# Pinning two weight-block sums behind the SwiGLU hand-over and moving the write-out of the residual stream

## The chip, the cores and the metric

The kernel runs on one core of a Trainium2 chip. The metric is device time in microseconds (us), the median over runs of the same program. One execution was also recorded by the hardware profiler; its own time is in the table below.

## The reference, cut to what matters

A trunk of two layers over 512 tokens of width 1024. Each layer is a half-step SwiGLU, a mixing block with three kinds of attention, and a second half-step SwiGLU. Every sub-layer sits between two RMS norms and adds to a residual stream `h`:

```python
def _swiglu(t, w_gate, w_up, w_down):
    return (jax.nn.silu(t @ w_gate) * (t @ w_up)) @ w_down
...
for l in range(DEPTH):                       # DEPTH = 2
    f = _swiglu(_rmsnorm(h, ffn1_pre_g[l]), ffn1_w_gate[l], ffn1_w_up[l], ffn1_w_down[l])
    h = h + 0.5 * _rmsnorm(f, ffn1_post_g[l])
    ...                                      # token mixing: h = h + _rmsnorm(merged @ w_out[l], mix_post_g[l])
    f = _swiglu(_rmsnorm(h, ffn2_pre_g[l]), ffn2_w_gate[l], ffn2_w_up[l], ffn2_w_down[l])
    h = h + 0.5 * _rmsnorm(f, ffn2_post_g[l])
```

The hidden width is 2816, 22 tiles of 128. Everything is float32.

## The kernel before, in words

**Products in three passes.** Each float32 operand is split into a high part (`wh`, `uh`: a cast on ACT, L180) and a low part (`wl`, `ul`: the rest, a subtraction on DVE, L181). A product is three matmul passes: high by high (L206), high by low (L207), low by high (L208). A weight block comes from DRAM into a `raw` tile by an SP DMA, then ACT makes its high part and DVE its low part. At most four high and four low weight tiles are live.

**A SwiGLU.** There are four, named a0, c0 (layer 0) and a1, c1 (layer 1). Each begins with the "first pair", hidden tiles 16 and 17, worked by `halved` in two halves over the tokens: the first half (tokens 0 to 255) starts as soon as token tiles 0 and 1 are normed and turned, the second (tokens 256 to 511) waits for tiles 2 and 3. Within a half, each weight is first used with the high part of the input (L639) and then with the low part (L636, L637). This second half is the hand-over.

After it the first 16 hidden tiles are worked as two chunks of seven block products each, for the gate (G), then the up weights (U). The seven products of a chunk use block-wise sums of inputs and of weights, in the order 0, 2, 1, 3, 4, 5, 6 (`ORDER`); each has two weight units (`k` = 0 and 2). A `BlockUnit` of product 2, 3, 5 or 6 needs a sum of two weight blocks first: one DVE `tensor_tensor` over 128x1024 (L316). For product 2 a second block is also fetched into a tile of the tag "o" that stays (`keep`; shown as `tga`, `tgc`, `tua`, ...).

The input side has sums too (`sums`, tiles `x..`, then `u` pairs), run on DVE beside the second half and the first four products.

**The chain to the second half.** For each token tile: residual add (L547), square sum on ACT, norm scale (L554), eight transposes on PE (L564), then the high part on ACT and the low part on DVE (L183, L184, tile `us_..`).

**Order.** The program is traced in the order the Python code runs, and a scheduler, which simulates the chip, then orders each engine's stream: an instruction goes when the simulation has its inputs ready, with the earlier traced one first among those that are ready. On the chip each engine then takes its stream in that order. `tc.keep_in_program_order(ins)` adds an edge that keeps `ins` behind the instruction traced last before it on the same engine. It adds no wait for a result.

At the start of the second half, `Q.load_ahead()` loads the next four units: the two of product 0 and the two of product 2 of chunk G 0. `Q.pinned` is true for that call, and `split` then pins the ACT cast and the DVE low part of each unit. The sum at L316 of product 2's units, traced just ahead of its cast, is not pinned.

**The tag "o" and the residual stream.** `h` lives in four of eight tiles of the tag "o". `leave()` writes the four tiles to DRAM (`park`, L650; not in a0, where `h` is still the input), and sets `RINGS["o"]` to 4, which lets `fetch_ahead` request weight blocks into the freed tiles. The write is read back at the SwiGLU's end.

The lines that the change touches lie in `BlockUnit.load` and in `halved`:

Of the kernel before, what the change touches and what calls it, by code (L numbers as in the profile page):

```python
# [13 lines left out]
ALU = mybir.AluOpType  # L14
# [8 lines left out]
def kernel(  # L23
# [38 lines left out]
    nc = tc.nc  # L62
# [47 lines left out]
    def pbank(tag, name):  # L110
        return ps.tile([P, S], F32, tag=tag, bufs=4, name=name)
# [121 lines left out]
    class Unit:  # L233
# [19 lines left out]
        def load(self):  # L253
            if self.h is not None:
                return
            self.fetch()
            self.split_from(self.raw[:])
            self.loaded()
# [16 lines left out]
    class BlockUnit(Unit):  # L275
# [31 lines left out]
        def load(self):  # L307
            if self.h is not None:
                return
            self.fetch()  # L310
            src = raw = self.raw[:]
            if self.n in (2, 3, 5, 6):
                t = self.keep.get(self.k0)
                src = raw if self.n == 5 else t
                a, b = (t, raw) if self.n in (2, 5) else (raw, t)
                nc.vector.tensor_tensor(src, a, b, ALU.subtract)  # L316
            self.split_from(src)
            self.loaded()

# [130 lines left out]
    Q = Queue()  # L450
# [138 lines left out]
    def ffn(l, src, wg, wu, wd, dst, name, spare, parked, plan, aside=None):  # L589
# [17 lines left out]
        def hidden(f, pg, pu):  # L607
            s = tmp(f"s{name}_{f}")
            nc.scalar.activation(s[:], pg[:], AF.Silu)
            if f < f0:  # L610
                nc.vector.tensor_tensor(hidden_rows(2 * f // FC)[:, f % (FC // 2)], pu[:], s[:], ALU.mult)
                return
            nc.vector.tensor_tensor(s[:], pu[:], s[:], ALU.mult)
            hid[f] = blk(tags[f - f0], f"hid{name}_{f}")
            split(hid[f][:, 0], hid[f][:, 1], s[:])
            if f == NF - 1:
                tc.keep_in_program_order(nc.scalar.preload_act_table_set("natural_log_exp_and_others"))

        def halved(f, ug, uu, half):
            if half == 0:  # L620
                st["p"] = [pbank("mm", f"p{x}{name}_{f + m}") for x in "gu" for m in range(2)]
            else:
                Q.hold, Q.pinned = False, True
                Q.load_ahead()
                Q.pinned = False
            c = HALVES[half]

            for uns, pts in ((ug, st["p"][:2]), (uu, st["p"][2:])):
                for low in (False, True):
                    for un in uns:  # L630
                        for k, (m, pt) in itertools.product(range(un.nk), enumerate(pts)):
                            kk, cols = un.k0 + k, slice(m * P, (m + 1) * P)
                            wh, wl = un.h[:, k, cols], un.l[:, k, cols]
                            ah, al = act(kk, c)
                            if low:
                                nc.tensor.matmul(pt[:, c], wh, al, start=False, stop=False, skip_group_check=True)  # L636
                                nc.tensor.matmul(pt[:, c], wl, ah, start=False, stop=kk == ND - 1, skip_group_check=True)  # L637
                            else:
                                nc.tensor.matmul(pt[:, c], wh, ah, start=kk == 0 and half == 0, stop=False, skip_group_check=True)  # L639
                            yield (1 + low) * S // 2 * PE_US  # L640
            if half == 1:
                for m in range(2):
                    hidden(f + m, st["p"][m], st["p"][2 + m])
                leave()

        def leave():

            if parked is not None:
                for t in range(NT):
                    nc.sync.dma_start(parked[t], hT[t][:])  # L650
            RINGS["o"] = 4
            Q.fetch_ahead()
# [206 lines left out]
        def first_pair():  # L859
            ug, uu = plain(f0)  # L860
            some = st["some"] = sums()
            marks["early"] = ug + uu
            for un, place in zip(ug + uu, ("tri", "tri", (spare, spare), (spare, spare))):
                un.tags = place
            Q.add(ug + uu, lambda: halved(f0, ug, uu, 0), src.ready((0, 1)))
            Q.add([], lambda: beside(halved(f0, ug, uu, 1), itertools.islice(some, 4), 12), src.ready(range(NT)))
            marks["first"] = len(Q.jobs)
# [751 lines left out]
```

## Time and profile before

| what | value |
|---|---|
| median of 3 runs | 2428.29 us (2422.43 to 2429.78) |
| profiled execution: its own time, its span | 2429.58 us, 2427.8 us |
| PE (matmul) busy | 2392.5 us, 99% |
| PE weight loads busy | 2134.2 us, 88% |
| DVE busy | 1870.4 us, 77% |
| ACT busy | 1365.0 us, 56% |
| DMA | 372.12 MB, mean 153 GB/s |

The span is the time from the first to the last instruction of the profiled execution. "Busy" is the time in which the engine has at least one instruction running. A row of the timeline is: start, duration, engine, line, operation, tile written <- tiles read, shapes, count, and in square brackets the engine's idle time before it with what ended it. SPq is the DMA queue of SyncE: there the duration is that of the issue, not of the transfer.

In the profiled execution the second halves of the four hand-overs start at about 27.4 us (a0), 884.2 us (c0), 1234.4 us (a1) and 2089.4 us (c1).

### The profile page before, as it was taken

How to read it: one execution, taken by the hardware profiler on the slowest of the kernel's cores; microseconds unless marked ns; L12 is line 12 of the kernel's file. 1: busy time of each engine (PE TensorE's matmuls, PEld its weight loads, DVE VectorE, ACT ScalarE, POOL GpSimd, SP SyncE). 2: the span in 40 equal slices, each digit the busy share in tenths (PEclk: the TensorE clock that was granted, in tenths of full speed). 3: DMA queues.
4: the chain of work that ended last, by engine and by line, in shares of the span. 5: the costliest groups of instructions: out<-in, count | busy, mean ns of one | idle time of the engine just before them, and what ended most of it. 6: DMA issues, size and time to landing. Idle time of an engine off the chain costs nothing.

```text
span 2427.8 us, 36744 instructions
## 1 busy us (share of the span) xinstructions
PE 2392.5 (99%) x14471; PEld 2134.2 (88%) x14471; DVE 1870.4 (77%) x2500; ACT 1365.0 (56%) x2201; POOL 70.9 (3%) x124
## 2 busy tenths in 40 slices
PE   9999999999999999999999999999999999999998
PEld 8998888888888889998899988888888888999886
DVE  8878876678776688788797788766778766887885
ACT  6555565567655555455554544655676655545544
POOL 0000000000110000000000000000001100000000
PEclk9999999999999999999999999999999999999999
DMA  6765454222223466655556655542232234576544
GB/s 235 225 195 186 157 192 138 77 72 70 79 70 113 153 203 196 213 175 177 193 187 215 198 184 173 185 118 70 71 87 75 65 129 150 190 230 196 177 158 151
DMA packets 249345, 372.12 MB, mean 153 GB/s; under 512 B 11450, under 2 KB 126162, under 8 KB 249172
## 3 DMA queue, kind: packets, MB, share of 16 engines
q1 hardware_dynamic: 249076, 369.74, 47.4%
q8 instruction: 114, 1.87, 0.3%
q14 instruction: 59, 0.48, 0.1%
q0 software_dynamic: 96, 0.03, 0.0%
HBM read 357.14 MB, written 12.58 MB: 152 GB/s over the span
## 4 chain that ended last, share of the span: by engine, by line
PE 78%; DVE 8%; DMA 7%; ACT 4%; issue 2%; SPq 0%; DVEq 0%; ACTq 0%
PE pg L206 3%; PE pg L207 3%; PE pg L208 3%; PE pdc L207 3%; PE pdc L206 2%; PE pdc L208 2%; PE pda L207 2%; PE pda L208 2%; PE pda L206 2%; PE pb L208 2%; PE pb L206 2%; PE pb L207 2%; DMA raw_da<-in_ffn_w_down_dram 1%; PE pwc0g L206 1%; PE pwc0g L207 1%
## 5 line engine op out<-in xcount | busy, mean ns | idle before, releaser
L206 PE MATMUL pg<-us_a,wh_wg 128*128 128x512 f32 x384 | 150.9, 393 | 0.0
L207 PE MATMUL pg<-us_a,wh_wg 128*128 128x512 f32 x384 | 150.0, 391 | 0.0
L208 PE MATMUL pg<-us_a,wl_wg 128*128 128x512 f32 x384 | 149.8, 390 | 0.0
L207 PE MATMUL pda<-wl_da,aha 128*128 128x512 f32 x224 | 87.5, 391 | 2.7 <-DVE wl_da L181 2.7
L207 PE MATMUL pdc<-wl_dc,ahc 128*128 128x512 f32 x224 | 87.6, 391 | 0.0
L208 PE MATMUL pdc<-wh_dc,alc 128*128 128x512 f32 x224 | 87.2, 389 | 0.0
L208 PE MATMUL pda<-wh_da,ala 128*128 128x512 f32 x224 | 87.2, 389 | 0.0
L206 PE MATMUL pda<-wh_da,aha 128*128 128x512 f32 x224 | 86.5, 389 | 0.0
L206 PE MATMUL pdc<-wh_dc,ahc 128*128 128x512 f32 x224 | 86.5, 389 | 0.0
L181 DVE TENSOR_TENSOR wl_dc<-raw_dc,wh_dc 128x1024 fp32r<-128x1024 f32 x50 | 61.1, 1222 | 32.2 <-ACT wh_dc L180 31.8
L208 PEld LDWEIGHTS pg<-us_a,wl_wg 128*128 128x128 f32 x384 | 72.4, 188 | 15.3
L206 PEld LDWEIGHTS pg<-us_a,wh_wg 128*128 128x128 f32 x384 | 72.4, 189 | 14.5
L207 PEld LDWEIGHTS pg<-us_a,wh_wg 128*128 128x128 f32 x384 | 72.4, 189 | 14.4
L180 ACT CAST wh_dc<-raw_dc 128x1024 fp32r<-128x1024 f32 x50 | 52.6, 1053 | 56.1 <-PE pdc L208 17.2
L184 DVE SCALAR_TENSOR_TENSOR wl_wg<-raw_wg,wh_wg 128x1024 fp32r<-128x1024 f32 x48 | 58.7, 1222 | 30.1 <-ACT wh_wg L183 29.8
L181 DVE TENSOR_TENSOR wl_da<-raw_da,wh_da 128x1024 fp32r<-128x1024 f32 x50 | 61.1, 1222 | 24.8 <-ACT wh_da L180 24.3
L180 ACT CAST wh_da<-raw_da 128x1024 fp32r<-128x1024 f32 x50 | 52.6, 1053 | 47.2 <-PE pda L208 19.7
L180 ACT CAST wh_uc<-raw_uc 128x1024 fp32r<-128x1024 f32 x44 | 46.2, 1049 | 50.7 <-PE pwc1u L207 10.7
L181 DVE TENSOR_TENSOR wl_uc<-raw_uc,wh_uc 128x1024 fp32r<-128x1024 f32 x44 | 53.7, 1221 | 24.7 <-ACT wh_uc L180 24.1
L180 ACT CAST wh_ua<-raw_ua 128x1024 fp32r<-128x1024 f32 x44 | 46.0, 1048 | 44.7 <-PE pwa1u L207 12.5
L181 DVE TENSOR_TENSOR wl_ua<-raw_ua,wh_ua 128x1024 fp32r<-128x1024 f32 x44 | 53.4, 1220 | 20.7 <-ACT wh_ua L180 19.9
L183 ACT ACTIVATE wh_wg<-raw_wg 128x1024 fp32r<-128x1024 f32 x48 | 51.0, 1062 | 28.2 <-PE pv L1043 16.2
(639 smaller groups left out, 8954.6 us busy)
## 6 DMA issues: line engine op xcount, KB each, us to landing
raw_da<-in_ffn_w_down_dram SPq DMA_DIRECT2D x74, 512.0 KB, 5.1
raw_dc<-in_ffn_w_down_dram SPq DMA_DIRECT2D x74, 512.0 KB, 4.8
raw_ga<-in_ffn_w_gate_dram SPq DMA_DIRECT2D x68, 512.0 KB, 4.6
raw_ua<-in_ffn_w_up_dram SPq DMA_DIRECT2D x68, 512.0 KB, 4.4
raw_gc<-in_ffn_w_gate_dram SPq DMA_DIRECT2D x68, 512.0 KB, 4.0
raw_uc<-in_ffn_w_up_dram SPq DMA_DIRECT2D x68, 512.0 KB, 4.3
raw_wg<-in_w_gate_dram SPq DMA_DIRECT2D x48, 512.0 KB, 3.6
raw_wo<-in_w_out_dram SPq DMA_DIRECT2D x24, 512.0 KB, 3.6
```

Source lines behind the costliest of these rows:

```text
L180: both = [nc.scalar.copy(h_ap, src)]
L181: make = lambda: nc.vector.tensor_tensor(l_ap, src, h_ap.bitcast(F32), ALU.subtract)
L183: both = [nc.scalar.activation(h_ap, src, AF.Copy, scale=scale)]
L184: make = lambda: nc.vector.scalar_tensor_tensor(l_ap, src, scale, h_ap.bitcast(F32), ALU.mult, ALU.subtract)
L206: nc.tensor.matmul(pt, lh, rh, start=start, stop=False, skip_group_check=free)
L207: nc.tensor.matmul(pt, lh, rl, start=False, stop=False, skip_group_check=free)
L208: nc.tensor.matmul(pt, ll, rh, start=False, stop=stop, skip_group_check=free)
```

## The change

Two edits. The sum of two weight blocks is pinned when `Q.pinned` is true, as the cast and the low part already are. And `leave()` is traced at the start of the second half, ahead of `Q.load_ahead()`, and no longer at its end.

```diff
@@ BlockUnit.load
                 a, b = (t, raw) if self.n in (2, 5) else (raw, t)
-                nc.vector.tensor_tensor(src, a, b, ALU.subtract)
+                ins = nc.vector.tensor_tensor(src, a, b, ALU.subtract)
+                if Q.pinned:
+                    tc.keep_in_program_order(ins)
             self.split_from(src)
@@ halved
             if half == 0:
                 st["p"] = [pbank("mm", f"p{x}{name}_{f + m}") for x in "gu" for m in range(2)]
             else:
+                leave()
                 Q.hold, Q.pinned = False, True
                 Q.load_ahead()
                 Q.pinned = False
@@ halved, at its end
             if half == 1:
                 for m in range(2):
                     hidden(f + m, st["p"][m], st["p"][2 + m])
-                leave()
```

## The prediction

> **What bounds the kernel now.** I read the page first, then the waits of PE, then the four hand-overs in the timeline, then windows over the stretch behind each.
>
> ```profile
> PE 2392.5 (99%) x14471; PEld 2134.2 (88%) x14471; DVE 1870.4 (77%) x2500; ACT 1365.0 (56%) x2201; POOL 70.9 (3%) x124
> ```
>
> PE sets the time: about 35 us of the span of 2427.8 are left in which it does nothing. A change that removes no matmul can win only what PE waits, and what a slow clock costs. At the hand-overs it waits here (PE, then DVE, in the timeline; c0, c1, a1):
>
> ```profile
> 889.06 0.38 PE L636 MATMUL pgc<-us_b,w_gc 128*128 128x256 f32 x1 [2.65 <-DVE us_b L184]
> 2093.19 0.39 PE L636 MATMUL pgc<-us_b,w_gc 128*128 128x256 f32 x1 [1.61 <-DVE us_b L184]
> 1228.81 0.41 PE L564 MATMUL utc<-ident,fc 128*128 128x128 f32 x2 [1.20 <-DVE nhc L470]
> ...
> 882.24 1.22 DVE L316 TENSOR_TENSOR tgc<-tgc,raw_gc 128x1024 f32<-128x1024 f32 x1
> 883.38 1.28 DVE L184 SCALAR_TENSOR_TENSOR us_b<-utb,us_b 128x512 fp32r<-128x512 f32 x2
> 887.17 1.23 DVE L316 TENSOR_TENSOR tgc<-tgc,raw_gc 128x1024 f32<-128x1024 f32 x1 [2.52 <-DMA tgc<-in_ffn_w_gate_dram]
> 888.32 1.28 DVE L184 SCALAR_TENSOR_TENSOR us_b<-utb,us_b 128x512 fp32r<-128x512 f32 x2
> ...
> 1226.24 1.23 DVE L316 TENSOR_TENSOR tga<-tga,raw_ga 128x1024 f32<-128x1024 f32 x1 [0.99 <-DMA raw_ga<-in_ffn_w_gate_dram]
> 1227.38 1.28 DVE L554 SCALAR_TENSOR_TENSOR fc<-hfc,nhc,gqc 128x1024 f32<-128x1024 f32 x1
> ```
>
> In c0 the second sum of the block weights (L316) stands in DVE's stream ahead of the low parts of token tile 3 (`us_b` at 888.32) and waits there 2.52 us for its own DMA. PE's low matmuls stand behind those low parts. In a1 the sum at 1226.24 stands ahead of tile 2's norm scale (L554), which PE's transposes need. So one cause shows three times: an early sum blocks a later, urgent instruction. a0 has the sum too, but no PE wait behind it (below).
>
> **The sums: what PE can gain.** With the pin the two sums come behind the low parts of product 0's units, which stand behind tile 3's low parts already, so none can stand ahead of `us_..`. Windows from the second half's first matmul to the start of its up weights (length first, granted clock third from the right; c0, c1, a1, then the slow part of c0):
>
> ```profile
> 884.20:894.50 10.30, 7.61 (x49) 7.41 (x50) 7.78 (x9) 5.69 (x7) 0.00 (x0) 0.83 0.75 226
> 2089.40:2097.30 7.90, 6.28 (x50) 6.08 (x51) 6.41 (x8) 5.71 (x7) 0.00 (x0) 1.00 0.71 224
> 1234.30:1240.20 5.90, 5.85 (x49) 5.85 (x49) 5.87 (x7) 5.59 (x7) 0.00 (x0) 1.00 0.41 127
> 889.00:894.40 5.40, 5.34 (x32) 5.35 (x33) 5.40 (x7) 1.76 (x2) 0.00 (x0) 0.68 0.80 232
> ```
>
> The same 48 matmuls take 5.9 us in a1, where nothing blocks `us_c`. So c0 can gain 10.3 - 5.9 = 4.4 us, c1 7.9 - 5.9 = 2.0; a1 gains its wait of 1.2; a0 nothing. That is a ceiling of 7.6 us. The 4.4 is more than the wait of 2.65: after it the clock was granted at 0.68 for 5.4 us, which costs 0.32 x 5.4 = 1.7 more. After the 1.61 of c1 it stayed at 1.00.
>
> [...]
>
> **The sums: what DVE gives back.** The sums are moved, not removed, and DVE behind the hand-over has no room. Windows from the end of tile 3's low parts to the low part of U 0's first weight unit (a0, c0, a1, c1; DVE busy is the fourth number):
>
> ```profile
> 28.95:76.01 47.06, 45.96 (x383) 45.76 (x383) 45.72 (x54) 34.10 (x42) 2.77 (x4) 1.00 0.65 212
> 889.60:934.88 45.28, 45.28 (x367) 45.28 (x366) 43.92 (x42) 24.05 (x29) 0.00 (x0) 0.96 0.61 200
> 1235.62:1281.02 45.40, 45.30 (x378) 45.09 (x376) 43.95 (x42) 27.36 (x34) 0.00 (x0) 1.00 0.45 143
> 2093.73:2138.55 44.82, 44.12 (x368) 43.91 (x366) 43.66 (x43) 24.94 (x30) 0.00 (x0) 1.00 0.62 204
> ```
>
> DVE idles 1.3, 1.4, 1.4 and 1.2 us in these 45 us. And PE meets DVE at their end:
>
> ```profile
> 931.39 2.35 DVE L316 TENSOR_TENSOR tuc<-tuc,raw_uc 128x1024 f32<-128x1024 f32 x2
> 933.66 1.22 DVE L181 TENSOR_TENSOR wl_uc<-raw_uc,wh_uc 128x1024 fp32r<-128x1024 f32 x1
> ...
> 935.04 0.28 PE L208 MATMUL pwc0u<-us_b,wl_uc 128*128 128x256 f32 x1
> ...
> PE pwa0u L206 <- ACT wh_ua L180: 1.1, 1, 1.1
> PE pwc1u L208 <- DVE wl_uc L181: 0.8, 1, 0.8
> PE pwa1u L208 <- DVE wl_ua L181: 0.2, 1, 0.2
> ```
>
> In c0 the low part ends at 934.88 and its matmul starts at 935.04; in a0, a1 and c1 PE already waits there. So up to this point the hand-over gains no more than DVE's stream moves forward. Two sums back to back take 933.66 - 931.39 = 2.3 us of that stream, which lay in its idle time before tile 3's low parts and now lie behind. How much earlier the low parts come is read against ACT, which makes their high parts (a1 is the free case; c0, c1, a1, a0):
>
> ```profile
> 883.59 1.08 ACT L183 ACTIVATE us_b<-utb 128x512 fp32r<-128x512 f32 x2 [2.05 <-PE utb L564]
> 2088.76 1.09 ACT L183 ACTIVATE us_b<-utb 128x512 fp32r<-128x512 f32 x2 [2.07 <-PE utb L564]
> 2092.45 1.28 DVE L184 SCALAR_TENSOR_TENSOR us_b<-utb,us_b 128x512 fp32r<-128x512 f32 x2
> 1233.70 1.08 ACT L183 ACTIVATE us_c<-utc 128x512 fp32r<-128x512 f32 x2 [3.14 <-PE utc L564]
> 1234.33 1.29 DVE L184 SCALAR_TENSOR_TENSOR us_c<-utc,us_c 128x512 fp32r<-128x512 f32 x2 [2.57 <-ACT us_c L183]
> 26.71 1.09 ACT L183 ACTIVATE us_x<-utx 128x512 fp32r<-128x512 f32 x2 [4.83 <-PE utx L564]
> 27.67 1.28 DVE L184 SCALAR_TENSOR_TENSOR us_x<-utx,us_x 128x512 fp32r<-128x512 f32 x2
> ```
>
> Free, DVE follows ACT by 1234.33 - 1233.70 = 0.63. So c0's low parts can start at 884.22 and not 888.32 (4.1 earlier), c1's at 2089.39 and not 2092.45 (3.1), a0's 0.3 earlier; a1's move with PE by 1.2. Less 2.3 each: c0 +1.8, c1 +0.8, a1 -1.1, a0 -2.0, together -0.5 us: a small loss. Against it, a stream that PE waits for closes idle time: at most all of the 1.3 + 1.4 + 1.4 + 1.2 = 5.3 us, which gives a gain of 4.8. I take half, since part of that idle time hangs on PE, which comes earlier, and part on DMAs, which don't: c0 +2.5, c1 +1.4, a1 -0.4, a0 -1.3, a gain of 2.2 us. Each is below its ceiling from PE.
>
> **What waits behind the pinned sums.** ACT's cast of product 2's units and DVE's low parts of them; then, as far as the simulation lets nothing pass, the input sums. The one round trip the trace shows is this:
>
> ```profile
> 888.43 1.05 ACT L180 CAST wh_gc<-tgc 128x1024 fp32r<-128x1024 f32 x1 [0.94 <-DVE tgc L316]
> ```
>
> From the sum's end at 888.40 to the cast's end at 889.48 are 1.1 us, twice per hand-over, since the second sum is pinned behind the first unit's low part. I count it at nothing: the input sums over `us_b` are ready then and are not pinned, so the scheduler can fill in. Without that cover it is the second rival.
>
> **The residual stream.** `leave()` issues four writes on SP in c0, a1 and c1 (none in a0), and its `fetch_ahead` the block fetches on the same queue; nothing of it is on POOL, ACT or DVE.
>
> ```profile
> 878.84 0.34 SPq L650 DMA_DIRECT2D park<-hm  x1
> 883.20 0.37 SPq L294 DMA_DIRECT2D tgc<-in_ffn_w_gate_dram  x1
> 883.68 0.41 SPq L294 DMA_DIRECT2D raw_gc<-in_ffn_w_gate_dram  x1
> ...
> 903.24 1.06 ACT L180 CAST wh_gc<-raw_gc 128x1024 fp32r<-128x1024 f32 x1 [1.63 <-PE pwc0g L207]
> ```
>
> The last write goes out at 878.84, 5.4 us ahead of the second half at 884.2, though it is traced behind it: it only waits for the residual add. Its landing frees the tile for the `keep` block at 883.20. Tracing it earlier changes none of these waits, and the fetches behind it are the same in the same order. Product 1's first block, fetched at 883.68 into a tile that the first sum frees, will be fetched some 5 us later, when that sum now ends; its cast at 903.24 waits for PE, not for the fetch. So I count nothing, between a gain and a loss of 4 x 0.34 = 1.4 us of SP issue time per hand-over, were the order on SP to turn.
>
> **Rivals.** First, the full gain: the scheduler, with the sums out of the way, orders DVE so that the low parts PE meets come ahead of sums needed later. The row at 931.39 speaks for it: two sums for U's product 2 stand ahead of the low part that PE needs at once. Against it: the same order came out in c0 and c1. Gain 7.6 us, 2420.7.
>
> Second, slower: the pinned chain sum, cast, low part, sum, cast, low part runs with nothing between, and DVE idles 2 x 1.1 = 2.2 us in each hand-over. Then c0 is -0.4, c1 -1.4, a1 -3.3, a0 -4.2, together 9.3 us lost, or 6.6 with the half of the idle time closed: 2434.9 to 2437.6. It decides where the input sums are already done or not ready when the first sum ends; nearest to it is a0, whose constants and input sums run first.
>
> Third, the pin moves nothing in the real stream, or as much is lost as won: 2428.3.
>
> **How the numbers follow.** The profiled execution took 2429.58 us, 1.8 more than its span and 1.3 more than the median of 2428.29. The span should become 2427.8 - 2.2 = 2425.6, and the median of runs 2426.1; the forecast's own range is 2423.5 to 2428.8. A measurement of this kernel tells about 0.3% (7.3 us) from no change: faster means below 2421.0, slower above 2435.6.
>
> Chances: the forecast 0.43 (0.04 of it faster, 0.39 within), the full gain 0.30 (0.20 faster, 0.10 within, since 2420.7 lies on the edge and the scheduler may shift other streams a little), the alternating chain 0.22 (0.16 slower, 0.06 within), nothing 0.05 (0.01 faster, 0.02 within, 0.02 slower). That is 0.25, 0.57 and 0.18. The range goes from 2418 (the full gain, and 2.7 below it for the scatter of runs, which spans 7 us) to 2437.
>
> **What would show it.** Right: L316 on `tgc<-tgc` behind the `us_..` low parts at all four hand-overs; no PE wait on `us_b L184`; clock 1.00 there in c0; second halves of 5.9 us; and a PE wait on U 0's `wl_u..`/`wh_u..` that grows in each SwiGLU, most in a0. The first rival: that wait gone or unchanged, and DVE's `tu.` sums behind `wl_u.`. The second: DVE idle 1 us before `wl_g.<-tg.` with ACT `wh_g.` as releaser, twice per hand-over. Wrong: PE waits of a new kind, on DMA blocks of product 1 or 3, or a different order on SP between `park` and the fetches.

## The result, and the profile after

The changed kernel takes 2415.1 us (median of 8 runs, 2410.15 to 2418.79) against 2425.98 us of the kernel before (median of 8, 2422.43 to 2429.78): 10.9 us less, ratio 0.9957, 95% interval 0.9945 to 0.9968. The prediction was 2426.1 in a range from 2418 to 2437, so the gain is five times the forecast's 2.2 us. The interval, 7.8 to 13.3 us, lies just above the 7.6 us that the prediction called a ceiling.

The profiled execution after took 2410.15 us, 4.95 below its own median, while that of before lay 3.6 above its median. So 8.5 of the 19.4 us between the two spans are the scatter of executions. The two traces can't simply be subtracted; what follows is read hand-over by hand-over. Page of the changed kernel, span, busy time and chain:

```profile
span 2408.4 us, 36758 instructions
...
PE 2385.7 (99%) x14471; PEld 2130.9 (88%) x14471; DVE 1871.3 (78%) x2500; ACT 1365.9 (57%) x2201; POOL 70.9 (3%) x124
...
PE 87%; DVE 6%; DMA 3%; ACT 2%; issue 1%; SPq 0%; DVEq 0%; ACTq 0%
```

PE is idle for 2408.4 - 2385.7 = 22.7 us, where it was 35.3. The waits of PE (in all, times, longest):

```profile
PE pts L1082 <- ACT ts L1111: 5.0, 2, 2.6
PE utc L566 <- DVE fc L556: 2.6, 1, 2.6
PE pda L207 <- DVE wl_da L181: 2.0, 3, 0.9
PE warm L1483 <- DVE warm L1575: 1.2, 1, 1.2
```

The waits for `us_b L184` are gone, and so are those for `wl_u..` and `wh_u..` at U 0. Windows over the second half of c0, c1, a1 and a0, from its first matmul to the first of its up weights:

```profile
877.14:882.99 5.85, 5.85 (x49) 5.85 (x50) 5.85 (x7) 3.64 (x5) 0.00 (x0) 1.00 0.49 131
2074.70:2080.55 5.85, 5.85 (x48) 5.85 (x49) 5.85 (x7) 3.64 (x5) 0.00 (x0) 1.00 0.37 112
1221.42:1227.27 5.85, 5.85 (x48) 5.85 (x49) 5.85 (x7) 3.64 (x5) 0.00 (x0) 1.00 0.22 59
26.48:32.27 5.79, 5.79 (x50) 5.79 (x49) 5.53 (x13) 2.26 (x3) 1.16 (x1) 1.00 0.82 307
```

All four take the 5.8 to 5.9 us of an undisturbed one, at a granted clock of 1.00. DVE in c0, from tile 3's low parts on:

```profile
877.12 1.29 DVE L184 SCALAR_TENSOR_TENSOR us_b<-utb,us_b 128x512 fp32r<-128x512 f32 x2 [0.89 <-ACT us_b L183]
878.32 1.22 DVE L688 TENSOR_TENSOR x10c<-us_b 128x1024 f32<-128x1024 f32 x1
879.46 2.36 DVE L181 TENSOR_TENSOR wl_gc<-raw_gc,wh_gc 128x1024 fp32r<-128x1024 f32 x2
881.73 1.22 DVE L316 TENSOR_TENSOR tgc<-tgc,raw_gc 128x1024 f32<-128x1024 f32 x1
882.86 1.22 DVE L688 TENSOR_TENSOR x11c<-us_b 128x1024 f32<-128x1024 f32 x1
...
886.27 1.22 DVE L181 TENSOR_TENSOR wl_gc<-tgc,wh_gc 128x1024 fp32r<-128x1024 f32 x1
887.40 1.22 DVE L316 TENSOR_TENSOR tgc<-tgc,raw_gc 128x1024 f32<-128x1024 f32 x1
```

The low parts start 0.63 us after ACT's high parts (which start at 876.49), as in the free case of before, the two sums stand behind product 0's low parts, and other ready work fills the time of the cast between a sum and its low part: input sums (L688) behind the first, a low part of the input side and a product of the first pair behind the second, with no idle time shown. Now the stretch from the end of tile 3's low parts to U 0's first low part (a0, c0, a1, c1):

```profile
27.69:72.47 44.78, 44.78 (x375) 44.78 (x374) 44.52 (x52) 29.03 (x37) 2.76 (x4) 1.00 0.58 187
878.41:923.24 44.83, 44.83 (x376) 44.83 (x375) 44.66 (x43) 27.18 (x33) 0.00 (x0) 1.00 0.64 208
1222.69:1267.52 44.83, 44.83 (x376) 44.83 (x375) 44.66 (x44) 27.19 (x33) 0.00 (x0) 1.00 0.48 151
2075.97:2120.81 44.84, 44.84 (x376) 44.84 (x375) 44.67 (x44) 27.19 (x33) 0.00 (x0) 1.00 0.61 199
```

PE is busy for all of it, so it is PE's own work that sets these 44.8 us. DVE idles 0.2 to 0.3 us (44.83 - 44.66 in c0) instead of 1.2 to 1.4. At its end DVE reads:

```profile
920.88 1.22 DVE L316 TENSOR_TENSOR tuc<-tuc,raw_uc 128x1024 f32<-128x1024 f32 x1
922.02 1.22 DVE L181 TENSOR_TENSOR wl_uc<-raw_uc,wh_uc 128x1024 fp32r<-128x1024 f32 x1
...
924.51 1.23 DVE L181 TENSOR_TENSOR wl_uc<-raw_uc,wh_uc 128x1024 fp32r<-128x1024 f32 x1
925.65 1.22 DVE L316 TENSOR_TENSOR tuc<-tuc,raw_uc 128x1024 f32<-128x1024 f32 x1
```

Before, both sums of the up side's product 2 stood ahead of the low part that PE meets. Now one stands ahead and one behind, in a1 and c1 too; in a0 both are behind.

Setting the start of each matmul after against the same one before gives the gain by hand-over: a0 1.4 us, c0 4.4, a1 1.7, c1 2.8, in all 10.3, which is the 10.9 us of the medians within their scatter. a0 is counted from 26 us on. The changed trace is 0.45 us ahead by 14.6 us already, but the first instruction with another place in the order comes only at 23 us, so that is scatter; the expectations below, with 1.9 us for a0 and 10.4 in all, count it in. Of the remaining 9 us between the two traces, the largest pieces (at 117, 229, 383 and 396 us, together 5.2) lie in places whose instruction order did not change.

### The profile page after: what moved, and what is told of

Read it like the earlier page. It is cut to its first block, busy times and chain, and to the rows that moved or that the text cites. A ratio compares the mean times of both kernels' runs of the same rounds, so it can differ in the third digit from the quotient of the medians.

```text
span 2408.4 us, 36758 instructions
## 1 busy us (share of the span) xinstructions
PE 2385.7 (99%) x14471; PEld 2130.9 (88%) x14471; DVE 1871.3 (78%) x2500; ACT 1365.9 (57%) x2201; POOL 70.9 (3%) x124
## 4 chain that ended last, share of the span: by engine, by line
PE 87%; DVE 6%; DMA 3%; ACT 2%; issue 1%; SPq 0%; DVEq 0%; ACTq 0%
PE pg L206 3%; PE pg L207 3%; PE pg L208 3%; PE pdc L207 3%; PE pdc L208 3%; PE pdc L206 3%; PE pda L207 2%; PE pda L208 2%; PE pda L206 2%; PE pb L208 2%; PE pb L206 2%; PE pb L207 2%; PE pwo L207 1%; PE pwo L206 1%; PE pwo L208 1%; DMA raw_da<-in_ffn_w_down_dram 1%
## 5 line engine op out<-in xcount | busy, mean ns | idle before, releaser
L184 DVE SCALAR_TENSOR_TENSOR wl_wg<-raw_wg,wh_wg 128x1024 fp32r<-128x1024 f32 x48 | 58.7, 1222 | 30.2 <-ACT wh_wg L183 29.9
L180 ACT CAST wh_da<-raw_da 128x1024 fp32r<-128x1024 f32 x50 | 52.7, 1053 | 46.2 <-PE pda L208 19.4
```

Of the source, the lines that this page charges most:

```text
L180: both = [nc.scalar.copy(h_ap, src)]
L184: make = lambda: nc.vector.scalar_tensor_tensor(l_ap, src, scale, h_ap.bitcast(F32), ALU.mult, ALU.subtract)
```

## The experiments

Each ratio is to the kernel before on the same chip, with its 95% interval.

**Which of the two edits.** First the sums pinned, `leave()` left where it was:

```diff
-                nc.vector.tensor_tensor(src, a, b, ALU.subtract)
+                ins = nc.vector.tensor_tensor(src, a, b, ALU.subtract)
+                if Q.pinned:
+                    tc.keep_in_program_order(ins)
```

> The sums kept in program order, the residual write left where it was. Theory A (the pinned sums carry the whole gain, 1.9 us at a0, 4.2 at c0, 1.5 at a1 and 2.8 at c1, 10.4 in all): the ratio to the kernel before is 0.9957 (0.9945 to 0.997), and TensorE waits for no us_ tile at any hand-over. Theory B (the earlier residual write carries part of it, by freeing the queue or the tiles ahead of the second half): at least 3 us of the 10.9 are missing, 0.997 or more.

Measured: 0.9959 (0.9946 to 0.9971). The order on PE, DVE, ACT and POOL is that of the full change; on SP one block fetch and one write of the residual are exchanged at c0, a1 and c1. The four stretches are 44.8 us again, and no wait for tile 3's low parts of `us_` is left. Theory A holds. The other edit alone:

```diff
             else:
+                leave()
                 Q.hold, Q.pinned = False, True
...
-                leave()
```

> The residual write ahead of the second half, the sums left free. Theory A: 1.000 (0.999 to 1.001), with the waits of 2.65 us at c0 and 1.61 us at c1 for us_b still there. Theory B: 0.9988 or less, that is 3 us or more gained without the pin.

Measured: 1.0003 (0.9994 to 1.0012), nothing gained. The free sum blocks in c0 once more, only a place earlier: DVE holds it for its DMA ahead of the norm scale, so the wait is PE's for `fb` this time, and the expected 2.65 us for `us_b` shows as 1.95 here. In c1 the expected 1.61 us shows as 0.54 for `fb` and 0.62 for `us_b`, and the wait for `wl_uc` at U 0 rises from 0.76 to 1.68 us. DVE, then PE, in c0:

```profile
880.57 1.23 DVE L316 TENSOR_TENSOR tgc<-tgc,raw_gc 128x1024 f32<-128x1024 f32 x1 [1.51 <-DMA raw_gc<-in_ffn_w_gate_dram]
...
883.34 1.06 PE L564 MATMUL utb<-ident,fb 128*128 128x128 f32 x8 [1.95 <-DVE fb L554]
```

**One hand-over alone.** The kernel before with the pin in a0 only:

```diff
+                if Q.pinned and self.name.startswith('ga0'):
+                    tc.keep_in_program_order(ins)
```

> The kernel before with the pin at a0's hand-over alone. Theory A: 1.9 us gained, ratio 0.9992 (0.9987 to 0.9997), with the activation-table loads at 67 to 79 us of the kernel before gone from that place. Rival (what a0 showed was scatter between executions): 1.0000 (0.9997 to 1.0003) and the waits near 19, 26 and 75 us still there.

Measured: 0.9990 (0.9981 to 0.9998), that is 2.4 us. The interval is too wide to tell 1.4 us from 4, but it excludes that nothing was gained, and the prediction had a0 losing 1.3. The trace, set against that of before from 26 us to U 0, gives 1.4 us again. The kernel before has six loads of an activation table on ACT between 67 and 80 us, three of them ahead of U 0's first cast. Here the first load of that stretch comes at 79.6 us, behind U 0, and the wait of 1.10 us for `wh_ua` is gone. Is that the loads, or DVE? The next kernel moves the loads and leaves the sums at the hand-over where they were:

```diff
-            nc.scalar.activation(ss[:, 1:2], ss[:, 0:1], AF.Ln)
+            tc.keep_in_program_order(nc.scalar.activation(ss[:, 1:2], ss[:, 0:1], AF.Ln))
```

> The kernel before with the Ln activations of mem_norm kept in program order, which takes ScalarE's table loads out of the stretch from 60 to 80 us and leaves the sums as they were. Theory A2 (1.24 us of a0's gain came from these loads having moved, not from the sums themselves): the wait of 1.10 us of TensorE for wh_ua at unit 0 of a0 is gone, while the waits near 19 and 26 us, 0.5 us each, stay. Rival (the sums at the hand-over decide it through VectorE): the wait of about 1.1 us at unit 0 stays.

Measured, in a single run: 2428.07 us, and the wait for `wh_ua` is gone; U 0 starts at 73.62 instead of 74.79, 1.2 us earlier. So of a0's gain some 1.2 us can be had without the pin, with the loads of 1.28 us each gone from there. Three of them stood in ACT's stream ahead of the cast that U 0 needed, and the pin moved them as a by-product of the new order. The loads were not the only thing that moved, though: in this kernel too the second sum of the up side stands behind U 0's low part (73.33 against 72.20 us), and its DVE does not wait for the block of that sum. What the loads are worth alone is not shown.

**How much room DVE has.** The changed kernel with each pinned sum followed by one more operation that leaves it as it is:

```diff
                 if Q.pinned:
                     tc.keep_in_program_order(ins)
+                    tc.keep_in_program_order(nc.vector.tensor_tensor(src, src, src, ALU.max))
```

> The changed kernel with one more VectorE operation of 128x1024 (a maximum of the sum with itself, which changes nothing, about 1.2 us) behind each pinned sum: two at each hand-over, eight in all. Theory C (VectorE's backlog up to unit 0 has no slack left, so that what the sums push back is paid again at unit 0): 2.3 us come back at each of the four, 9 us in all, and the ratio is 0.9995 (0.9985 to 1.0005), with a wait of about 2 us at unit 0's first low part. Theory D (the scheduler closes the backlog: other work that is not due is put behind unit 0's low part, as it did with the second sum): the stretch from the end of the us_ low parts to unit 0 stays within 0.5 us of 44.8 us at all four, and the ratio is 0.9957 to 0.997.

Measured: 1.0005 (0.9996 to 1.0014). All of the gain is lost, as theory C has it, but not where it said. The stretches of a0, c0, a1 and c1, and the rows on PE and DVE in c0:

```profile
27.29:75.49 48.20, 45.47 (x377) 45.06 (x376) 47.94 (x54) 28.99 (x37) 2.76 (x4) 1.00 0.58 187
886.69:933.46 46.77, 45.15 (x377) 44.95 (x375) 46.77 (x45) 26.73 (x33) 0.00 (x0) 1.00 0.63 204
1235.85:1282.62 46.77, 45.15 (x376) 44.95 (x375) 46.77 (x46) 26.74 (x33) 0.00 (x0) 1.00 0.48 148
2092.39:2139.16 46.77, 45.16 (x377) 44.96 (x376) 46.77 (x46) 26.73 (x33) 0.00 (x0) 1.00 0.60 196
...
920.81 1.22 DVE L181 TENSOR_TENSOR ulc<-x11c,uhc 128x1024 fp32r<-128x1024 f32 x1
922.08 0.38 PE L207 MATMUL pwc0g<-ulc,wh_gc 128*128 128x256 f32 x1 [1.62 <-DVE ulc L181]
...
118.46 0.39 PE L208 MATMUL pwa0g<-us_x,wl_ga 128*128 128x256 f32 x1 [2.25 <-DVE wl_ga L181]
1323.96 0.38 PE L208 MATMUL pwa1g<-us_c,wl_ga 128*128 128x256 f32 x1 [0.62 <-DVE wl_ga L181]
2180.48 0.38 PE L208 MATMUL pwc1g<-us_b,wl_gc 128*128 128x256 f32 x1 [0.60 <-DVE wl_gc L181]
```

DVE has no idle time left in c0, a1 and c1, and of 2.3 us more they lose 46.77 - 44.9 = 1.9 in this stretch, at an input of the gate side's products, not at U 0. a0 loses 3.4. PE also waits at the next block of weights (the last three rows; in c0 0.41). Only in a0 is that more than scatter: kernels without the extra work have waits of 0 to 0.7 us there in c0, a1 and c1 as well. Half of the extra work, behind the second sum only:

```diff
+                    if self.k0 == 2:
+                        tc.keep_in_program_order(nc.vector.tensor_tensor(src, src, src, ALU.max))
```

> The changed kernel with one more VectorE operation of about 1.2 us at each hand-over, behind the second pinned sum only. With two of them, 2.3 us of work lengthened the stretch from the us_ low parts to unit 0 by 1.9 us at c0, a1 and c1, and TensorE waited for ulc or ula, not for unit 0. Theory I (VectorE had 0.4 us left ahead of that input in the changed kernel): 1.15 - 0.4 = 0.75 us comes back at each hand-over, the stretch is about 45.65 us instead of 44.9, with a wait of 0.5 to 0.8 us for ulc; about 3 us in all, ratio 0.9969 (0.9957 to 0.998). Rival (the scheduler's other order with two operations made the wait, and the room is larger): 44.9 us at all four and 0.9957.

Measured: 0.9975 (0.9965 to 0.9984), nearly the predicted ratio, and again not in the predicted places:

```profile
28.52:77.92 49.40, 46.91 (x377) 46.50 (x375) 47.34 (x53) 28.72 (x37) 2.76 (x4) 0.97 0.57 181
889.50:934.40 44.90, 44.90 (x377) 44.90 (x376) 44.76 (x43) 26.98 (x33) 0.00 (x0) 1.00 0.62 201
1234.98:1279.88 44.90, 44.90 (x377) 44.90 (x376) 44.76 (x43) 26.96 (x33) 0.00 (x0) 1.00 0.47 144
2088.65:2133.55 44.90, 44.90 (x377) 44.90 (x375) 44.77 (x43) 26.96 (x33) 0.00 (x0) 1.00 0.60 193
```

c0, a1 and c1 take 1.15 us more without any loss, with other work again put behind the low part: theory I falls there, and its rival holds. Only a0 loses. Of its 49.40 us 1.7 are a slow clock that followed its waits in this execution (3.4 us at 0.50, hence the mean of 0.97), which leaves a loss of 2.9 us, about as much as with twice the work (48.20, a loss of 3.4). So the cost of pushed-back work is no fixed amount. In three of four places 1.15 us cost nothing and 2.3 us nearly all of it; in a0 1.15 us cost more than itself, and why a0 has no room was not followed.

Then the U sums of product 2 pinned as well, on top of the sums done twice:

```diff
-                if Q.pinned:
+                if Q.pinned or self.name[0] == 'u' and self.n == 2:
                     tc.keep_in_program_order(ins)
```

> The kernel with the sums done twice, and the sums of the up side's product 2 kept in program order as well, which puts unit 0's two low parts ahead of one more of them. Theory H (what VectorE can put behind unit 0's low part decides how much of a hand-over's pushed-back work is paid): 1.1 us less is paid at each of the four unit 0s than with the sums done twice alone, the stretch from the us_ low parts to unit 0 falls from 46.8 to about 45.6 us, and the ratio is 0.9986 (0.9975 to 0.9998). Rival (unit 0 is bound by ScalarE's casts or by the landing of the up weights): the stretch stays at 46.8 us and the ratio at 1.0005.

Measured: 0.9986 (0.9977 to 0.9996), the expected ratio, but not by the expected way. A window of c0, then a row of a0:

```profile
884.93:931.71 46.78, 45.16 (x377) 44.96 (x375) 46.16 (x44) 26.75 (x33) 0.00 (x0) 1.00 0.63 204
...
118.03 0.38 PE L208 MATMUL pwa0g<-us_x,wl_ga 128*128 128x256 f32 x1 [1.25 <-DVE wl_ga L181]
```

The stretch to U 0 is as long as without this pin, so theory H falls: U 0's low part was not what PE waited for. Between the two traces the wait at the next block is shorter: 2.25 us became 1.25 in a0, 0.60 became 0.19 in c1, those of c0 and a1 (0.41 and 0.62) are gone, and a0's drop of the clock (0.50 from 120.6 to 123.8 us with the sums done twice, below) did not come: here it stays at 1.00 from 112 to 132 us. That adds up to 4 of the 4.6 us between the two ratios, but it is one execution against one, and waits of 0 to 0.7 us come and go there between executions of one order. What brought the ratio back is not settled.

**The clock.** The changed kernel with 4, 5 and 6 more operations ahead of tile 3's low parts in c0, a1 and c1 (in the edit `b0`, `c0` and `b1`, the chains that lead to them), to lengthen PE's wait:

```diff
+                if hf == 0 and t == NT - 1:
+                    for _ in range({'b0': 4, 'c0': 5, 'b1': 6}.get(self.name, 0)):
+                        tc.keep_in_program_order(nc.vector.tensor_tensor(self.fs[t][:], self.fs[t][:], self.fs[t][:], ALU.max))
```

> The changed kernel with four (c0), five (a1) and six (c1) more VectorE operations of about 1.2 us, which change nothing, ahead of tile 3's low parts. TensorE should wait about 2.5, 3.6 and 4.8 us for us_ at the three hand-overs. Theory E (the length of the idle decides on the granted clock, and the bound lies between the 2.56 us that a1 waited at 1.00 and the 2.65 us that c0 of the kernel before waited before 0.68): the second halves of a1 and c1 run at 0.6 to 0.7 for some 5 us and take 7.2 us or more instead of 5.9, c0's stays at 1.00. [...]

Measured, in a single run: 2441.28 us. The waits came out 3.82, 5.08 and 6.34 us, longer than planned, and all three were followed by a clock of 0.50 (c0, the time after it, a1, c1):

```profile
885.10:891.80 6.70, 5.73 (x25) 5.36 (x26) 4.77 (x6) 3.76 (x4) 0.00 (x0) 0.50 0.09 9
891.90:895.20 3.30, 3.30 (x30) 3.30 (x30) 2.87 (x3) 1.14 (x2) 0.00 (x0) 1.00 0.96 342
1240.00:1246.80 6.80, 5.07 (x22) 4.70 (x23) 4.87 (x5) 3.76 (x4) 0.00 (x0) 0.50 0.00 0
2100.20:2110.40 10.20, 6.26 (x28) 5.89 (x29) 8.20 (x8) 3.76 (x4) 0.00 (x0) 0.50 0.09 15
```

The slow stretches last 6.8, 6.8 and 10.2 us. They begin 3.4 us after the wait of c0 began (881.57), 4.0 after that of a1 and 3.1 after that of c1. Theory E's bound between 2.56 and 2.65 us does not exist: other runs have a clock of 0.50 behind a wait of 1.71 us and of 1.00 behind one of 2.84 (last section).

**The wait that is left at a1.** The changed kernel with a1's first up units in another ring of tiles:

```diff
+            if name == 'a1':
+                for un in uu:
+                    un.place = 'v'
```

> The changed kernel with a1's up units of the first pair fetched into another ring of tiles. Theory G (the wait of 2.6 us that is left ahead of a1's transpositions comes from VectorE standing at wl_ua, whose weights land late because their tile comes free late): that wait falls under 0.7 us and the ratio to the kernel before is 0.995 (0.9937 to 0.9962). Rival (the norm's own chain is as long): the wait stays above 2 us, 0.9957.

Measured: 0.9937 (0.9925 to 0.9949), with this wait left:

```profile
1210.09 1.09 PE L566 MATMUL utc<-ident,fc 128*128 128x128 f32 x8 [1.05 <-DVE fc L556]
```

2.6 us became 1.05: less than theory G wanted, more than its rival allows. The next two kernels ran side by side, the change unaltered, and the ring with the U sums pinned:

> The changed kernel unaltered, beside the next one on the same chip: 0.9957 (0.9945 to 0.9968). It is there to tell whether the variant with another ring for a1's up units (0.9937) is faster than the change itself: then this one stays 2 us or more above it; if the two were the same, this one comes out at 0.9937 to 0.995 as well.

> The changed kernel with a1's up units of the first pair in the other ring and the sums of the up side's product 2 in program order as well. If the ring takes the wait of 2.6 us ahead of a1 to about 1.1 us and the pin brings nothing where TensorE doesn't wait at unit 0: 0.9937 to 0.9950, the same as with the ring alone; if putting unit 0's low parts first has a gain of its own (as the ratio of 0.9986 against 1.0005 with the sums done twice would have it, though the stretch to unit 0 was the same 46.8 us): 0.992 or less.

Measured: 0.9955 (0.9943 to 0.9967) for the change, 0.9942 (0.9930 to 0.9954) for the ring with the pin. The change repeats its first ratio. The pin adds nothing to the ring. Both variants with the ring have the lower ratio and the shorter wait (1.05 and 1.2 us against 2.2 to 2.6), but the intervals overlap: the ring is the best version run, faster than the kernel before for certain, and by the ratios 3 to 5 us faster than the change, which the intervals do not settle.

## Why the prediction was wrong, point by point

**What the sums block: right.** The low parts of tile 3 come 4.1 us earlier in c0 against PE's second half (they end 1.27 us behind its start, before 5.4), as worked out. The second halves take 5.85 us, the clock stays at 1.00 there, and the gain before U 0 is the ceiling: 10.3 - 5.85 = 4.4 in c0, 7.9 - 5.85 = 2.0 in c1, 1.2 in a1. Of c0's 4.4 us 1.7 are the slow clock, which does not follow every wait of that length (last section); behind c0's wait it came in the kernel before (0.50 behind 2.65 us) and with `leave()` alone (0.50 behind 1.95 us).

**What DVE gives back: the step that failed.** The prediction put 2.3 us per hand-over onto DVE's stream up to U 0, let half of the idle time go against it, and came to a gain of 2.2 us. The stream gave back nothing: from the low parts to U 0 it takes 44.8 us in all four, where it took 47.06, 45.28, 45.40 and 44.82. In c0, a1 and c1 1.0 to 1.3 us of the 2.3 went into idle time, nearly all of it and not half, and one U sum of 1.1 us went behind U 0's low part. The two make up 2.1 to 2.4 us. The prediction named the second of these as its first rival, gave it 0.30, and held against it that c0 and c1 had come out alike before; with the sums pinned the order at U 0 changed in all four. Its reason for closing only half of the idle time was that part of it hangs on DMAs. In the kernel before, 0.68, 0.74 and 0.80 us of it in a0, a1 and c1 were indeed a wait for a DMA, but that of a sum of the up side for its own block, the same blocking that the change was made against (a0, c1):

```profile
72.99 1.22 DVE L316 TENSOR_TENSOR tua<-tua,raw_ua 128x1024 f32<-128x1024 f32 x1 [0.68 <-DMA tua<-in_ffn_w_up_dram]
2134.92 2.50 DVE L316 TENSOR_TENSOR tuc<-tuc,raw_uc 128x1024 f32<-128x1024 f32 x2 [0.80 <-DMA raw_uc<-in_ffn_w_up_dram]
```

In the new order no sum waits for its block in this stretch. A part of the idle time was thus of the order's making and went with it. In a0 the prediction also read the wait at U 0 as one for DVE, while its own row names ACT's cast (`wh_ua`).

**The ceiling: too low.** 7.6 us counted what PE loses in the second halves. The prediction's own rows showed 1.1 + 0.8 + 0.2 = 2.1 us of waits at U 0 in a0, c1 and a1, and it took these only as a sign that DVE is late. With the order changed they went as well: 7.6 + 2.1 = 9.7, and with 0.4 in a0 at 27 us it is 10.1 of the 10.3 that the traces show. That a0 could gain nothing was wrong by 1.4 us, of which some 1.0 is the wait for ACT's cast at U 0.

**The second rival did not occur**, since input sums and other ready work fill the cast's time, as the prediction had argued. With the sums done twice a kin of it does occur: an input of the gate side comes late by 1.6 us.

**The residual stream: right.** It is worth nothing (1.0003). The order on SP did turn by one fetch, at no price that shows (0.9959 without, 0.9957 with it).

## What to carry to other kernels

Where a scheduler orders an engine's stream, an operation pushed back there is not paid at its duration: count first what can still be put behind the next instruction that the bounding engine needs, and all idle time that has no fixed cause. Here 1.15 us more went in for nothing at three of four places and 2.3 us cost 1.9, so such room is real, small, and found only by adding work until it shows. And when a stream is reordered, the ceiling is the sum of all waits that hang on it, also those on which one doesn't mean to work.

## What the runs showed of the hardware

In these runs a wait of PE cost its length, or 1.7 us more (PE is busy for 7.61 us of c0's second half before and for 5.85 us after, with the same matmuls), and its length alone does not decide which. Waits of 2.17 us (a1 before), 2.56 (a1 after) and 2.84 (a1 with half the extra work) were followed by a clock of 1.00, but waits of 1.71 us (before, for `us_a` at 382.79), 1.95 (c0 with `leave()` alone), 2.25 (a0 with the sums done twice) and 2.65 (c0 before) by 0.50:

```profile
1213.00:1220.00 7.00, 4.16 (x23) 3.28 (x22) 7.00 (x13) 4.12 (x10) 0.00 (x0) 1.00 0.60 170
...
384.80:388.20 3.40, 3.40 (x10) 2.62 (x9) 1.65 (x2) 0.39 (x1) 0.00 (x0) 0.50 0.64 174
...
885.20:888.40 3.20, 3.20 (x17) 3.20 (x17) 2.82 (x4) 3.20 (x4) 0.00 (x0) 0.50 0.63 177
...
120.60:123.80 3.20, 3.20 (x17) 3.20 (x17) 1.39 (x2) 0.51 (x1) 0.00 (x0) 0.50 0.52 156
...
890.00:893.40 3.40, 3.40 (x19) 3.40 (x18) 3.40 (x4) 0.78 (x1) 0.00 (x0) 0.50 0.78 239
```

The rows are windows of a1 with half the extra work (with the 2.84 us wait inside), before behind the 1.71 us wait, c0 with `leave()` alone, a0 with the sums done twice, and c0 before: 3.4 us at half the clock, which the prediction read as 0.68 over 5.4. With longer waits the slow time was 6.8, 6.8 and 10.2 us. Before has three slow stretches between 13 and 2420 us, each of 3.413 us in the trace's record of the clock; windows of the 3.41 us ahead of each, then of the stretch:

```profile
381.40:384.81 3.41, 1.81 (x7) 1.25 (x8) 2.54 (x4) 2.97 (x5) 0.00 (x0) 1.00 0.57 158
384.81:388.23 3.41, 3.41 (x10) 2.63 (x9) 1.64 (x2) 0.38 (x1) 0.00 (x0) 0.50 0.63 175
...
886.57:889.99 3.41, 0.93 (x7) 0.93 (x8) 2.81 (x4) 2.46 (x3) 0.00 (x0) 1.00 0.47 137
889.99:893.40 3.41, 3.41 (x19) 3.41 (x18) 3.41 (x4) 0.80 (x1) 0.00 (x0) 0.50 0.79 239
...
1804.76:1808.17 3.41, 0.90 (x6) 0.48 (x6) 3.37 (x10) 2.00 (x5) 0.31 (x1) 1.00 0.00 0
1808.17:1811.58 3.41, 3.41 (x13) 2.98 (x12) 3.09 (x5) 2.89 (x7) 1.04 (x2) 0.50 0.00 0
```

PE was not idle for all of the 3.41 us ahead of a drop: it worked for 1.81, 0.93 and 0.90 us of them here, and for 1.41 of 3.40 us with `leave()` alone. The beginnings of the three stretches lie 505.18 and 918.18 us apart, 148.0 and 269.0 times 3.413; in the one run with three long waits those of the slow stretches lie 355.0 and 860.2 us apart, 104.0 and 252.0 times that. So in these two traces the drops lie on steps of 3.413 us, whatever the wait ahead of them. That where a wait falls against such steps counts beside its length is an estimate from these four distances; what decides was not shown. One wait more or fewer with such a stretch behind it moves a run by 1.7 us, part of the 7 to 9 us over which executions of one kernel scatter (2422.43 to 2429.78 before, 2410.15 to 2418.79 after).
